# A junk row and two residual rows placed anew at the end of the first attention of a two-layer diffusion trunk

## The chip, the cores and the metric

The kernel runs on one core of one Trainium2 chip, in one launch. The metric is the device time of that core in microseconds (us). Before the change it is 3322.68 us, the median of three runs (3320.38 to 3323.68).

## What is computed

Two layers of a trunk over 1024 latent tokens and 256 context tokens, width 1024, all in float32. Layer 0 mixes grouped-query attention with a bidirectional recurrence; layer 1 is a neighbourhood attention. Each mixer and each gated feed-forward network (a ConvFFN) sits between two RMS norms, with shift, scale and gate from the conditioning vector. The part around the change is the end of layer 0's mixer and the start of its feed-forward network:

```python
y_lat = jnp.concatenate([oa_lat, readout(ob_lat, bg_l)], axis=-1) @ w_out
x = x + g1 * rms_norm(y_lat, norm_post_mix[l])
h_lat = rms_norm(x, norm_pre_ffn[l]) * (1.0 + sc2) + sh2
u = h @ w_up
```

The same is done for the context rows (`ctx`, `h_ctx`). The output is the latent stream after both layers.

## The kernel before, in words

Products run on TensorE (PE) as three products each of operands split into a high and a low part, written in the names as h and l. The program is a row of stages, and each takes its tiles from pools in on-chip memory that are given back when the stage ends. A tile of a later stage that lies on bytes of an earlier one waits for the last instructions that use the earlier tile. In the attention and in the seam behind it the order of each engine, and of the queue of loads on SyncE (SP), is the order in which the code is written (`in_order`).

`even_attention` goes over five blocks of 256 rows, first the context and then four blocks of x, and over 8 heads each. For every pair of block and head, softmax weights `a_p` are computed, turned on PE (`transposes`, L1136) and split into `a_ph0`, `a_pl0`, `a_ph1` and `a_pl1` (halves of the keys), which `values` multiplies into `a_pv`; `finish` adds the two halves of a head by way of `pv_t` into `a_oT` (L1172). The context block has only the first half of the keys.

Between these, `project` multiplies finished blocks by `w_out`, and after the last head it has the engines for itself. For each 128 rows (row tiles 0 to 7 of x, 8 and 9 of the context), `y_half` evicts half a row at a time: a square on ACT with its sum (L354, into a junk row `yjunk`) and a copy on DVE (L355). Then follow the norm (L364), the residual row `y_x`, loaded by SP (L1216) and added (L1222), a store of the sum to `x1d` (L1224), a second square with sum by `squares` (L1191), the row times its inverse norm into `y_x` (L1229), and the store of that to `xnd` (L1230). The stores are issued by GpSimd (POOL). `y_x` has two buffers, so the residual load of row tile n+2 waits for the store of row tile n to `xnd`.

`ffn_up` follows. SP loads the normalised rows back as tiles `n_x` (L1611) in the order 8, 9, 0, 1, 2, 3, then the first two tiles of up-projection weights `w_raw` (L1530), then 4, 5, 6, 7, then the convolution's table `cw` (L1662). PE transposes `n_x` (L1344) into three banks in turn, ACT applies scale and shift (L1345) into `n_t` for the context and `x_t` for the rest, and DVE splits them (L1332, L1333) into `x_ctx` and `x_B` tiles. In the ACT order the first weight cast `w_A11h` (L1546) stands behind the sixth `n_t`; POOL makes its low part (L1547). The first product `u_g` needs four rows of x and these weights.

`squares` writes its squares, which nobody reads, to `sq_junk`, the last small tile at the attention pool's start. In the built program it lies at bytes 21376 to 22400 of each partition, and the place of the first `n_x` tile of the next stage is 20096 to 24192. `a_ph1` and `a_pl1` are each 5120 bytes long, and a row of 1024 values takes 4096.

Of the kernel before, what the change touches and what calls it, by code (L numbers as in the profile page):

```python
# [11 lines left out]
F32 = mybir.dt.float32  # L12
F32R = mybir.dt.float32r
BF16 = mybir.dt.bfloat16
AF = mybir.ActivationFunctionType
# [5 lines left out]
P = 128  # L21
D = 1024
# [17 lines left out]
LINE = 32  # L40
# [25 lines left out]
class Trunk:  # L66
# [958 lines left out]
    def even_attention(self, gp, tp, pp, sp):  # L1025
# [5 lines left out]
        nc, a = self.nc, self.a  # L1031
        QB = 2 * P
        blocks = [(SEQ, 1)] + [(QB * i, 0) for i in range(4)]
# [10 lines left out]
        def load_gate(kind):  # L1044
            g = st["gate"] = sp.tile([P, D], F32, name="gate", bufs=1)
            nc.sync.dma_start(g, self.gated[0, 0, kind].partition_broadcast(P))
# [140 lines left out]
                st["ready"] = b  # L1187

        def squares(y, ms):
            for h in range(2):  # L1190
                nc.scalar.activation(yjunk, y[:, 512 * h:512 * h + 512], AF.Square, scale=1.0 / 32.0, accum_out=ms[:, h:h + 1])  # L1191

        late = []

        def project():

            for b, (n0, kind) in enumerate(blocks):
                for i in range(2):
                    y = sp.tile([P, D], F32, name="y", bufs=2)
                    ms = self.small.tile([P, 2], F32, name="y_ms")  # L1200
                    for half in range(2):
                        ps = gp.tile([P, 512], F32, name="g_ps")
                        for k in range(KT):
                            xhk, xlk = (o[:, i * P:(i + 1) * P] for o in st["o", b, k])
                            whk, wlk = (w[:, 512 * (k % 2):512 * (k % 2) + 512] for w in W[4 * half + k // 2])
                            self.mm(ps, xhk, whk, k == 0, False)
                            self.mm(ps, xhk, wlk, False, False)
                            self.mm(ps, xlk, whk, False, k == KT - 1)
                            if late:
                                late.pop(0)()  # L1210
                            yield b
                        late.append(lambda ps=ps, y=y, ms=ms, half=half: self.y_half(ps, y, ms, half, sp))
                        if half == 0:
                            xt = sp.tile([P, D], F32, name="y_x", bufs=2)
                            r = n0 + i * P
                            nc.sync.dma_start(xt, a["ctx"][i * P:(i + 1) * P] if kind else a["x"][r:r + P])  # L1216
                        else:
                            late.append(lambda ms=ms: st.update(r=self.y_rstd(ms)))
                            late.append(lambda: None)
                            late.append(lambda: None)  # L1220
                            late.append(lambda y=y: self.y_norm(y, st["r"], st["gate"]))
                            late.append(lambda y=y, xt=xt: nc.vector.tensor_tensor(out=y, in0=y, in1=xt, op=OP.add))  # L1222
                            late.append(lambda: None)
                            late.append(lambda y=y, r=r: nc.gpsimd.dma_start(self.x1d[r:r + P], y))  # L1224
                            ms2 = self.small.tile([P, 2], F32, name="y_ms")
                            late.append(lambda y=y, ms2=ms2: squares(y, ms2))
                            late.append(lambda ms2=ms2: st.update(r2=self.y_rstd(ms2)))
                            late.append(lambda: None)
                            late.append(lambda y=y, xt=xt: nc.scalar.mul(xt, y, st["r2"]))  # L1229
                            late.append(lambda xt=xt, r=r: nc.gpsimd.dma_start(self.xnd[r:r + P], xt))  # L1230
                    if b == 0 and i == 1:
                        late.append(lambda: load_gate(0))
            while late:
                late.pop(0)()

        fill, todo, at = project(), [], [0]

        def step(n):
# [5 lines left out]
                elif late:  # L1244
                    late.pop(0)()

        zeros = sp.tile([P, 2 * LINE], F32, name="zeros", bufs=1)[:, 0:1]
        nc.vector.memset(zeros, 0.0)
        pv_t = sp.tile([P, QB], F32, name="pv_t", bufs=1)
        yjunk = sp.tile([P, 512], BF16, name="sq_junk", bufs=1)  # L1250
        N = 2 * len(pairs)
        later = {4: lambda: load_keys(0, 0), 6: lambda: load_keys(0, 1), 8: lambda: load_values(0, NT - 2),
                 10: lambda: load_keys(1, 0), 12: lambda: load_keys(1, 1), 14: lambda: load_gate(1)}
# [1614 lines left out]
```

## Time and profile before

| What | Value |
|---|---|
| Median of three runs | 3322.68 us |
| The profiled execution's own time | 3321.63 us |
| Its span, first to last instruction | 3319.9 us |
| Mean granted TensorE clock | 0.972 |
| Busy: PE, DVE, ACT, POOL | 3097.1, 2019.6, 1502.2, 1562.5 us |
| Main stretch of the first attention | 720 to 1027 us |
| Last projection block alone | 1027 to 1053 us |
| First transposes of the next stage | 1063 us |

The profile is one execution. Busy time is shown by engine; a matmul's end is modelled, so a busy PE isn't PE at its peak. The chain of waits follows the work that ended last back from the end, at each step to what released it. A row of the timeline has the start, the duration, the engine (PEld is the load of weights into PE), the line, the operation, and the tiles written and read; the bracket holds the idle time of that engine just before it and what ended it. A row of a table of waits has the total in us, how many times, and the longest.

### The profile page before, as it was taken

Reading aid. Unit: us, or ns where it says so; the run is one execution under the profiler, and the core shown is the slowest. Engines: PE = TensorE matmul, PEld = TensorE weight load, DVE = VectorE, ACT = ScalarE, POOL = GpSimd, SP = SyncE. Lnnn points to the kernel's source line nnn. Section 1 sums busy time; section 2 is a strip of 40 time slices with the busy share of each in tenths; the row PEclk is TensorE's granted clock in tenths of the full one; section 3 lists DMA queues with packets and bytes.
Section 4 is the critical chain, followed back from the end, with each engine's and each line's share of the span. In section 5 each row is a group of like instructions: output and inputs, shape, how many; then the busy total and the mean of one; then the engine's idle time right before and its main releaser. Section 6 shows DMA issues by size and latency. Waiting matters only on the chain.

```text
span 3319.9 us, 48782 instructions
## 1 busy us (share of the span) xinstructions
PE 3097.1 (93%) x18364; PEld 2547.6 (77%) x18364; DVE 2019.6 (61%) x3386; ACT 1502.2 (45%) x2681; POOL 1562.5 (47%) x1181
## 2 busy tenths in 40 slices
PE   7989999789997899999999989999998989999997
PEld 4766777478886688888878768898986768888785
DVE  4366666567774654554577862477775555555778
ACT  3232232366664543343344442566665434434443
POOL 1130111487773566666510111677764367777202
PEclk8999999889998899999999989999998989999998
DMA  6534311721114121211385772222224212222856
GB/s 249 197 103 133 119 49 38 271 73 60 48 61 153 41 76 69 75 67 66 108 288 195 264 229 107 73 63 61 63 81 155 90 64 88 84 77 89 281 179 218
DMA packets 203357, 398.73 MB, mean 120 GB/s; under 512 B 23521, under 2 KB 85473, under 8 KB 203121
## 3 DMA queue, kind: packets, MB, share of 16 engines
q1 hardware_dynamic: 192512, 358.89, 32.1%
q0 software_dynamic: 10608, 36.72, 2.9%
q8 instruction: 144, 2.36, 0.3%
q14 instruction: 93, 0.75, 0.1%
HBM read 316.86 MB, written 79.06 MB: 119 GB/s over the span
## 4 chain that ended last, share of the span: by engine, by line
PE 72%; DVE 11%; ACT 3%; DMA 3%; issue 3%; POOL 2%; SPq 0%; POOLq 0%; DVEq 0%; ACTq 0%
PE g_ps L136 18%; PE u_g L136 14%; PE d_ps L136 11%; PE u_v L136 10%; PE u_pc L136 4%; PE a_pv L136 2%; PE c_pv L136 2%; PE c_s L136 2%; PE c_pt L2503 2%; PE a_pt L1136 2%; DVE a_pl L1138 1%; PE o_ps L136 1%; PE a_s L136 1%; ACT a_ph L1137 1%; DMA d_rawB<-in_w_down 1%
## 5 line engine op out<-in xcount | busy, mean ns | idle before, releaser
L144 POOL TENSOR_TENSOR rs_r<-rs_e,mhalf 128x1 f32<-128x1 f32 (+3 forms) x106 | 85.7, 809 | 855.7 <-DVE rs_e L143 805.7
L136 PE MATMUL d_ps<-d_Bl,d_Ah 128*128 128x512 f32 x704 | 276.7, 393 | 4.1 <-DVE d_Bl L1874 3.5
L136 PE MATMUL d_ps<-d_Bh,d_Ah 128*128 128x512 f32 x704 | 275.5, 391 | 2.8 <-ACT d_Ah L1873 1.8
L136 PE MATMUL d_ps<-d_Bh,d_Al 128*128 128x512 f32 x704 | 275.7, 392 | 2.0 <-DVE d_Al L1874 1.9
L2486 POOL TENSOR_SCALAR c_p<-c_p,rl 128x640 f32<-128x640 f32 (+1 forms) x128 | 232.5, 1818 | 95.4 <-DVE rl L2485 61.8
L1116 POOL TENSOR_SCALAR a_p<-a_p,rl 128x1280 f32<-128x1280 f32 (+1 forms) x80 | 240.3, 3007 | 55.8 <-DVE rl L1115 49.5
L136 PE MATMUL g_ps<-xh,w_hi 128*128 128x512 f32 (+1 forms) x640 | 256.7, 401 | 5.6 <-DVE hq L748 3.5
L136 PE MATMUL g_ps<-xh,w_lo 128*128 128x512 f32 (+1 forms) x640 | 237.5, 371 | 1.3 <-POOL w_lo L2386 1.3
L136 PE MATMUL g_ps<-xl,w_hi 128*128 128x512 f32 (+1 forms) x640 | 237.7, 371 | 0.0
L1138 DVE TENSOR_TENSOR a_pl<-a_pt,a_ph 128x512 fp32r<-128x512 f32 (+1 forms) x200 | 119.0, 602 | 95.6 <-ACT a_ph L1137 95.5
L1561 DVE TENSOR_TENSOR f_u<-u_v,f_p 128x512 f32<-128x512 f32 x88 | 60.5, 688 | 183.7 <-PE u_v L136 183.7
L1547 POOL TENSOR_TENSOR w_S4l<-w_s,w_S4h 128x512 fp32r<-128x512 f32 x44 | 57.2, 1299 | 229.7 <-ACT w_S4h L1546 229.7
L136 PEld LDWEIGHTS d_ps<-d_Bl,d_Ah 128*128 128x128 f32 x704 | 132.7, 188 | 36.7 <-DVE d_Bl L1874 8.6
L136 PEld LDWEIGHTS d_ps<-d_Bh,d_Ah 128*128 128x128 f32 x704 | 132.8, 189 | 32.6 <-ACT d_Ah L1873 3.1
L136 PEld LDWEIGHTS d_ps<-d_Bh,d_Al 128*128 128x128 f32 x704 | 132.9, 189 | 30.0 <-DVE d_Al L1874 3.3
L1137 ACT CAST a_ph<-a_pt 128x512 fp32r<-128x512 f32 (+1 forms) x200 | 102.0, 518 | 108.6 <-PE a_pt L1136 108.5
L2506 DVE TENSOR_TENSOR c_pl<-c_pt,c_ph 128x256 fp32r<-128x256 f32 (+1 forms) x256 | 112.9, 470 | 57.9 <-ACT c_ph L2505 56.8
L136 PE MATMUL g_ps<-w_hi,xh 128*128 128x512 f32 (+1 forms) x368 | 143.2, 389 | 4.7 <-DVE xh L2260 2.1
L136 PEld LDWEIGHTS g_ps<-xh,w_hi 128*128 128x128 f32 x640 | 121.4, 190 | 31.0 <-issue 14.3
L136 PE MATMUL g_ps<-w_lo,xh 128*128 128x512 f32 (+1 forms) x368 | 137.6, 374 | 4.1 <-DVE w_lo L2247 2.9
L2505 ACT CAST c_ph<-c_pt 128x256 fp32r<-128x256 f32 (+1 forms) x256 | 98.4, 414 | 91.6 <-PE c_pt L2503 89.5
L136 PEld LDWEIGHTS g_ps<-xh,w_lo 128*128 128x128 f32 x640 | 121.0, 189 | 24.1 <-POOL w_lo L2386 1.7
(570 smaller groups left out, 9902.6 us busy)
## 6 DMA issues: line engine op xcount, KB each, us to landing
m_raw<-in_w_mod SPq DMA_DIRECT2D x96, 512.0 KB
w_raw<-in_w_up SPq DMA_DIRECT2D x88, 512.0 KB
d_rawA<-actd SPq DMA_DIRECT2D x77, 512.0 KB
d_rawB<-in_w_down SPq DMA_DIRECT2D x74, 512.0 KB
actd<-f_t SPq DMA_DIRECT2D x22, 640.0 KB
d_t<-in_w_down SPq DMA_DIRECT2D x22, 512.0 KB
actd<-f_t SPq DMA_DIRECT2D x22, 512.0 KB
d_s<-actd SPq DMA_DIRECT2D x20, 512.0 KB
```

The costliest lines, as they stand in the source:

```text
L136: return self.nc.tensor.matmul(out, lhsT, rhs, start=start, stop=stop, skip_group_check=True, **k)
L144: nc.gpsimd.tensor_tensor(out=r[:p, :n], in0=e[:p, :n], in1=self.mhalf[:p, :n], op=OP.pow)
L1116: nc.gpsimd.tensor_scalar(Pt[:, :nk], Pt[:, :nk], rl, None, op0=OP.mult)
L1136: nc.tensor.transpose(pt[:, m, qt * P:(qt + 1) * P], Pt[:, kts[j + m] * P:(kts[j + m] + 1) * P], self.ident)
L1137: nc.scalar.copy(ph[:, j:j + n], pt[:, :n])
L1138: nc.vector.tensor_tensor(out=pl[:, j:j + n], in0=pt[:, :n], in1=ph[:, j:j + n].bitcast(F32), op=OP.subtract)
L1547: nc.gpsimd.tensor_tensor(out=lo, in0=part(j, name), in1=hi.bitcast(F32), op=OP.subtract)
L1561: nc.vector.tensor_tensor(out=out, in0=x, in1=y, op=OP.add)
L2486: nc.gpsimd.tensor_scalar(Pt[:, :n], Pt[:, :n], rl, None, op0=OP.mult)
L2503: nc.tensor.transpose(pt[:, j, :], Pt[:, (src + j) * P:(src + j + 1) * P], self.ident)
L2505: nc.scalar.copy(vap(ph, o, dims), pt[:, :cnt])
L2506: nc.vector.tensor_tensor(out=vap(pl, o, dims), in0=pt[:, :cnt], in1=vap(ph, o, dims).bitcast(F32), op=OP.subtract)
```

## The change

Three edits, all in `even_attention`:

- `squares` no longer has a tile of its own. It takes the tile `yjunk`, the same that `y_half` takes, which lies at the pool's end (byte 153984).
- The residual rows of the last block, row tiles 6 and 7, are put in the places of `a_ph1` and `a_pl1` instead of in the two buffers of `y_x`.
- The tile `zeros` grows from 256 to 768 bytes. With `sq_junk` (1024 bytes) gone, `pv_t` moves up by 512 bytes, and all later tiles of this pool move down by 512.

```diff
         def squares(y, ms):
+            junk = sp.tile([P, 512], BF16, name="yjunk", bufs=1)
             for h in range(2):
-                nc.scalar.activation(yjunk, y[:, 512 * h:512 * h + 512], AF.Square, scale=1.0 / 32.0, accum_out=ms[:, h:h + 1])
+                nc.scalar.activation(junk, y[:, 512 * h:512 * h + 512], AF.Square, scale=1.0 / 32.0, accum_out=ms[:, h:h + 1])

         late = []
+
+        def row_place(b, i):
+            if b < len(blocks) - 1:
+                return sp.tile([P, D], F32, name="y_x", bufs=2)
+            return sp.tile([P, 5 * QB], F32, name="y_x", tag=f"a_p{'hl'[i]}1", bufs=1)[:, :D]
...
-                            xt = sp.tile([P, D], F32, name="y_x", bufs=2)
+                            xt = row_place(b, i)
...
-        zeros = sp.tile([P, 2 * LINE], F32, name="zeros", bufs=1)[:, 0:1]
+        zeros = sp.tile([P, 6 * LINE], F32, name="zeros", bufs=1)[:, 0:1]
...
-        yjunk = sp.tile([P, 512], BF16, name="sq_junk", bufs=1)
```

No instruction is added or removed, and none changes its place in the order of its engine. What changes is what the instructions wait for (and the line numbers behind the edit, by 5 or 6). In the rows below the bracket names the semaphores that an instruction waits for: an engine's own, or DMAHW and DMASW for the transfers that SP and POOL issue. A wait that the engine has already made by an earlier one isn't repeated.

The SP queue before, from the last two residual loads to the `n_x` loads of row tiles 4 and 5:

```order
L1216 DMA y_x<-in_x 128x1024 [waits DMAHW6_49,DMASW5_49,Activation_49]
L1216 DMA y_x<-in_x 128x1024 [waits DMAHW7_49,DMASW7_49,Activation_49]
L1611 DMA n_x<-xnd 128x1024 [waits DMAHW0_49,DVE_49,Activation_49]
L1611 DMA n_x<-xnd 128x1024 [waits DMAHW1_49,PE_49]
L1611 DMA n_x<-xnd 128x1024 [waits DMAHW2_49,Pool_49]
L1611 DMA n_x<-xnd 128x1024 [waits DMAHW3_49]
L1611 DMA n_x<-xnd 128x1024 [waits DMAHW4_49]
L1611 DMA n_x<-xnd 128x1024 [waits DMAHW5_49]
L1530 DMA w_raw<-in_w_up 128x1024 [waits DMAHW6_49,PE_49]
L1530 DMA w_raw<-in_w_up 128x1024 [waits DMAHW7_49]
L1611 DMA n_x<-xnd 128x1024 [waits DMAHW0_49]
L1611 DMA n_x<-xnd 128x1024 [waits DMAHW1_49]
```

The same piece of the SP queue now:

```order
L1222 DMA y_x<-in_x 128x1024 [waits DMAHW6_49,DVE_49,PE_49]
L1222 DMA y_x<-in_x 128x1024 [waits DMAHW7_49,PE_49]
L1616 DMA n_x<-xnd 128x1024 [waits DMAHW0_49,DVE_49]
L1616 DMA n_x<-xnd 128x1024 [waits DMAHW1_49]
L1616 DMA n_x<-xnd 128x1024 [waits DMAHW2_49,Pool_49]
L1616 DMA n_x<-xnd 128x1024 [waits DMAHW3_49]
L1616 DMA n_x<-xnd 128x1024 [waits DMAHW4_49]
L1616 DMA n_x<-xnd 128x1024 [waits DMAHW5_49]
L1535 DMA w_raw<-in_w_up 128x1024 [waits DMAHW6_49,PE_49]
L1535 DMA w_raw<-in_w_up 128x1024 [waits DMAHW7_49]
L1616 DMA n_x<-xnd 128x1024 [waits DMAHW0_49,DMASW5_49]
L1616 DMA n_x<-xnd 128x1024 [waits DMAHW1_49,DMASW7_49]
```

The two residual loads wait for DVE and PE (the last users of `a_ph1` and `a_pl1`) where they waited for the stores of row tiles 4 and 5 (DMASW5 and DMASW7) and for ACT. These two store waits have moved to the loads that read row tiles 4 and 5 back. The first `n_x` load doesn't wait for ACT any more.

ACT before, from the evictions of the last 128 rows to the second `n_t`:

```order
L354 ACTIVATE yjunk,y_ms<-g_ps 128x512 [waits PE_49]
L354 ACTIVATE yjunk,y_ms<-g_ps 128x512 [waits PE_49,Activation_49]
L1191 ACTIVATE sq_junk,y_ms<-y 128x512 [waits DVE_49]
L1191 ACTIVATE sq_junk,y_ms<-y 128x512 [waits Activation_49]
L1229 ACTIVATE y_x<-y,rs_r 128x1024 [waits DMAHW7_49,DMASW7_49,Pool_49]
L1345 ACTIVATE n_t<-n_pv,mod_3_1848,mod_4_3110 128x256 [waits PE_49]
L1345 ACTIVATE n_t<-n_pc,mod_3_1848,mod_4_3110 128x256 [waits PE_49]
```

The same piece of ACT now (x2 is two equal rows):

```order
L354 ACTIVATE yjunk,y_ms<-g_ps 128x512 [waits PE_49,Activation_49] x2
L1192 ACTIVATE yjunk,y_ms<-y 128x512 [waits DVE_49,Activation_49]
L1192 ACTIVATE yjunk,y_ms<-y 128x512 [waits Activation_49]
L1235 ACTIVATE y_x<-y,rs_r 128x1024 [waits DMAHW7_49,Pool_49]
L1350 ACTIVATE n_t<-n_pv,mod_3_1848,mod_4_3110 128x256 [waits DMASW1_49,PE_49]
L1350 ACTIVATE n_t<-n_pc,mod_3_1848,mod_4_3110 128x256 [waits PE_49]
```

Squares and evictions now wait for each other on ACT, since they write one junk row; over the whole program nine ACT instructions get such a wait. The first `n_t` waits for a store (DMASW1, the one of row tile 6 to `xnd`), since it lies on bytes of `a_ph1`, where that row is now. On POOL, the first two sums of weights of the next stage wait likewise for the stores of row tiles 6 and 7.

## The prediction, as it was put on record

> **What bounds the kernel now.** I read the page first, then the stages around the change, then the SP queue's waits, then the chain of waits in order of time, and last the single rows of ACT, DVE, PE and POOL at the one place where these meet.
>
> The page's head and a table by stage (length, then busy time and count of PE, weight loads, DVE, ACT, POOL, then the granted TensorE clock, the DMA share and GB/s):
>
> ```profile
> span 3319.9 us, 48782 instructions
> PE 72%; DVE 11%; ACT 3%; DMA 3%; issue 3%; POOL 2%; SPq 0%; POOLq 0%; DVEq 0%; ACTq 0%
> ...
> 720.00:1027.00 307.00, 284.49 (x1829) 246.65 (x1828) 223.65 (x419) 205.06 (x399) 228.12 (x109) 1.00 0.16 56
> 1027.00:1053.00 26.00, 25.76 (x114) 20.99 (x112) 10.05 (x18) 10.48 (x27) 8.64 (x14) 1.00 0.36 135
> 1053.00:1063.00 10.00, 0.00 (x0) 0.00 (x0) 3.73 (x7) 3.14 (x7) 2.24 (x4) 0.70 0.41 147
> 1063.00:1079.00 16.00, 10.89 (x43) 7.28 (x44) 8.66 (x19) 9.05 (x16) 2.54 (x2) 0.55 1.02 383
> 1130.00:1760.00 630.00, 624.67 (x3197) 534.48 (x3196) 339.59 (x372) 251.32 (x343) 348.15 (x250) 1.00 0.30 105
> ```
>
> TensorE carries 72% of the chain, and from 1130 on it is busy 624.67 of 630 us. The seam between the first attention and the first feed-forward is the exception: PE does nothing from 1053 to 1063, and then, with the DMA share at 1.02, half work at a granted clock of 0.55. The change touches only what comes before this seam, so the question is what the seam waits for. First the SP queue's waits from 1020 to 1110 (in total, times, longest):
>
> ```profile
> SPq L1216 <- DMA xnd<-y_x: 41.3, 2, 30.5
> SPq L1611 <- ACT sq_junk L1191: 15.8, 1, 15.8
> ```
>
> Two residual loads stand still until earlier normalised rows are stored; the third wait is one load of `n_x` (a normalised row tile of the next stage) that waits 15.8 us for `sq_junk`, whose contents nobody reads. In order of time SP, and the chain behind it, look so:
>
> ```profile
> 1031.96 11.55 SPq L1216 DMA_DIRECT2D y_x<-in_x  x2
> 1059.36 3.03 SPq L1611 DMA_DIRECT2D n_x<-xnd  x6
> 1062.49 10.65 DMA w_raw<-in_w_up
> 1074.28 1.02 DVE x_ctx3h L1332
> 1085.18 1.58 DVE x_B211l L1333
> 1086.81 1.81 PE u_g L136 x5
> ```
>
> Six `n_x` loads go out at 1059.36, right behind the last squares, the first up-projection weights at 1062.49 behind them, and their 10.65 us is the longest piece of the chain here. After that DVE alone carries it to 1086.8. ACT and PE, row by row (bracket: idle time and who ended it):
>
> ```profile
> 1049.59 1.15 ACT L1229 ACTIVATE y_x<-y,rs_r 128x1024 f32<-128x1024 f32 x1 [1.12 <-POOL rs_r L144]
> 1050.64 0.58 ACT L354 ACTIVATE yjunk<-g_ps 128x512 bf16<-128x512 f32 x1
> ...
> 1060.45 1.15 ACT L1229 ACTIVATE y_x<-y,rs_r 128x1024 f32<-128x1024 f32 x1 [1.12 <-POOL rs_r L144]
> 1065.23 0.56 ACT L1345 ACTIVATE n_t<-n_pv,mod,mod 128x256 f32<-128x256 f32 x1 [3.63 <-PE n_pv L1344]
> ...
> 1068.83 0.56 ACT L1345 ACTIVATE n_t<-n_pt,mod,mod 128x256 f32<-128x256 f32 x1
> 1073.16 0.62 ACT L1546 CAST w_A11h<-w_raw 128x512 fp32r<-128x512 f32 x1 [3.77 <-DMA w_raw<-in_w_up]
> 1073.69 0.56 ACT L1345 ACTIVATE n_t<-n_pv,mod,mod 128x256 f32<-128x256 f32 x1
> ```
>
> ```profile
> 1052.38 0.39 PE L136 MATMUL g_ps<-w_hi,a_ol 128*128 128x512 f32 x1
> 1063.20 0.45 PE L1344 MATMUL n_pv<-ident,n_x 128*128 128x128 f32 x1 [10.44 <-DMA n_x<-xnd]
> ```
>
> ACT stands idle twice, 3.63 us for transposes that wait for the late `n_x`, 3.77 us for the late weights. Those two holes are what this seam could give back.
>
> **The change, part by part.**
>
> *Junk row.* The squares now write the row that `y_half` uses, at the pool's end, and the first `n_x` tile no longer lies on a row that ACT writes last. In the new order that load waits for DVE alone: of what lies under its tile now (`zeros`, `pv_t`, a part of the keys), `pv_t` is read last, by the last `a_oT` add. The last two residual loads, now in `a_ph1` and `a_pl1`, wait for the last `a_pv` matmuls that read those tiles:
>
> ```profile
> 1026.62 0.28 PE L136 MATMUL a_pv<-a_pl,V 128*128 128x256 f32 x1
> 1027.34 0.42 DVE L1172 TENSOR_TENSOR a_oT<-a_pv,pv_t 64x256 f32<-64x256 f32 x1 [3.17 <-ACT pv_t L1170]
> ```
>
> So SP issues both residual rows at about 1026.9 and six `n_x` at 1027.8 (3.03 us for six issues). They were needed at 1063.2 and took 3.84 us to the first use (1059.36 to 1063.20); even ten times that is hidden under 26 us of projection, where DMA share is 0.36. Both parts are needed: with the junk row alone, SP would be stuck until about 1043 (1031.96 + 11.55) at the second residual load; with the rows alone, `n_x` would still wait for `sq_junk`. The 4 MB that come earlier delay no reader on the path, since PE reads only resident tiles here.
>
> *Weights.* The first two loads still wait for the last projection matmul, 1052.38 + 0.39 = 1052.8. They now stand first instead of behind six others. The worst price I have for them is the 10.65 above, under full DMA load: 1063.5.
>
> *First term.* PE's first transposes need `n_x`, which is there, and a bank that this copy empties:
>
> ```profile
> 1053.58 0.69 DVE L355 COPY y<-g_ps 128x512 f32<-128x512 f32 x1 [1.54 <-ACT yjunk L354]
> ```
>
> They can start at 1054.3 and finish long before ACT is free. ACT is in order and ends `y_x` at 1060.45 + 1.15 = 1061.60; at the same handover above the next instruction begins 0.10 before the end (1050.64 against 1050.74). The first `n_t` moves from 1065.23 to 1061.50: **3.73 us**.
>
> *Second term.* The sixth `n_t` then stands at 1065.10, and the weight cast directly behind it at 1065.10 + 0.56 - 0.10 = 1065.56 instead of 1073.16, since even the worst landing, 1063.5, is earlier. That is another 3.77 + 0.10 = **3.87 us**; together 7.60.
>
> *The collision with POOL.* The low half of the first weights (POOL) will fall nearer to DVE's context splits:
>
> ```profile
> 1069.76 0.42 DVE L1333 TENSOR_TENSOR x_ctx2l<-n_t,x_ctx2h 128x256 fp32r<-128x256 f32 x1
> 1075.32 1.52 DVE L1333 TENSOR_TENSOR x_ctx3l<-n_t,x_ctx3h 128x256 fp32r<-128x256 f32 x1
> ...
> 1073.87 1.26 POOL L1547 TENSOR_TENSOR w_A11l<-w_raw,w_A11h 128x512 fp32r<-128x512 f32 x1 [11.40 <-ACT w_A11h L1546]
> ```
>
> The same operation takes 0.42 alone and 1.52 beside POOL. POOL began 0.71 after the ACT cast, so it will begin at 1066.27, and `x_ctx2l` will run from 1066.03 (1069.76 less 3.73). The overlap costs between 0 and 1.10 us; I take 0.1, near the uncontended row, because DVE starts first. The Trainium skill, page "SBUF — State Buffer", section "Who interferes with whom", says that a VectorE instruction with two SBUF inputs and a GpSimd one that reads SBUF exclude each other, and that whichever issues first keeps the port until it ends. By that rule POOL would wait and the sum would stay at 7.60; by the stretched row alone it would be 6.50. The 1.52 beside POOL agrees with the exclusion; which of the two yields when DVE starts first, no row here shows.
>
> *Own-engine waits.* Sharing the junk row makes nine ACT rows wait for an earlier square on ACT itself. Price: the second square of a pair, which has such a wait already, starts after the one before it has ended, instead of 0.10 before:
>
> ```profile
> 1047.52 0.19 ACT L1191 ACTIVATION_READ_ACCUMULATOR sq_junk<-y 128x1 f32 x1
> 1047.74 0.63 ACT L1191 ACTIVATE sq_junk<-y 128x512 bf16<-128x512 f32 x1
> ```
>
> 1047.74 - 1047.71 + 0.10 = 0.13 us each, 1.2 for nine at most, 0 if other instructions lie between, which they do in the order at all nine. I take 0. Behind them on ACT stand casts of softmax weights, for which PE waits.
>
> *New waits on stores.* The first `n_t` now lies on the row-6 residual and waits until that row is stored; POOL's first sums wait for rows 6 and 7. Landing of these stores, and their issue:
>
> ```profile
> 1051.03 0.57 POOL L1230 DMA_DIRECT2D xnd<-y_x  x1 [1.48 <-ACT y_x L1229]
> 1061.89 0.57 POOL L1230 DMA_DIRECT2D xnd<-y_x  x1 [1.48 <-ACT y_x L1229]
> ...
> DMA to landing us min/median/max: 2.9/3.0/8.2
> ```
>
> Row 6 lands at 1054.0, by the worst store at 1059.2; both are before 1061.50, so the price is 0. If that cover were gone, every microsecond past 1061.50 would go straight into ACT. Row 7 lands at 1064.9 (1070.1 at worst); its `n_x` load is first read in the second half of the rows, where PE stands at
>
> ```profile
> 1082.43 0.60 PE L1344 MATMUL n_pc<-ident,n_x 128*128 128x128 f32 x4
> ```
>
> and 7.5 earlier is 1074.9: 1 us of slack even at worst (1070.1 + 3.84 = 1073.9).
>
> *Addresses.* Nearly all tiles of the attention move 512 bytes down. Nothing in the trace prices an address; I take 0.
>
> *Sum.* 3.73 + 3.87 - 0.1 = **7.5 us**. What follows the seam moves with it: DVE's share of the next stretch (busy time, count, clock, DMA)
>
> ```profile
> 1075.00:1090.00 15.00, 12.61 (x17) 0.84 0.37 144
> ```
>
> is nearly all of it up to 1086.8 (11.8 us), so what moves DVE's start moves PE's `u_g`, and from 1130 on PE is the bound and carries the shift to the end. The profiled execution took 3321.63 us (span 3319.9 and 1.73 around it), 1.05 under the median of the runs: 3321.63 - 7.5 = 3314.1, and from the median 3322.68 - 7.5 = **3315.2 us**.
>
> **Rivals.**
>
> *Only the first hole closes.* If the weights still land late, the cast waits as before: 3322.68 - 3.73 = 3319.0. For it: 10.65 us is a long landing, and DMA share was 1.02. Against: 3 MB of what filled it (six `n_x` of 512 KB) has gone before. Chance 0.08.
>
> *Nothing comes through.* DVE's splits, or the last row's `n_x`, set the seam's end: 3322.7. For it: that row's load needs the store after the last squares, which does not move. Against: 1 us of slack at the worst landing and 6 at the usual. Chance 0.06.
>
> *More than the sum.* PE at 0.55 of its clock runs a part of its 10.89 us in the seam faster, since its first transposes now stand before 1056; a quarter of 10.89 is 2.7, so 3312.5. Against: it will still idle some 6 us until 1061.5, and DVE is the bound there. Chance 0.08.
>
> *Slower: the new wait takes the place of the old.* The row-6 store now shares the DMA engines with the weights issued at 1052.8, and the first `n_t`, with all of ACT behind it, waits for it. It eats the gain when it lands later than 1061.5 + 7.5 = 1069.0, 18 us after its issue, and costs a microsecond for each one after that; at 25 us in flight the kernel takes 3329.7. Against: the slowest such store took 8.2 us, against six loads and two more. Chance 0.04.
>
> **How the numbers follow.** The forecast has 0.74, with its own range of 3313.4 to 3317.4: above, the collision's other end (1.0 more) and the nine waits (1.2); below, the collision's 0.1 and half of the 3.3 us by which the three runs differ. To leave out no more than 2 in 10 the range reaches to the partial gain and to the larger one: **3312.4 to 3319.1**. A measurement of this kernel can tell about 0.2% from no change, 6.6 us: the line is at 3316.0, only 0.8 above the forecast. Faster by more: three quarters of the forecast's 0.74 plus the 0.08 for more, rounded: 0.64. Within 0.2%: the rest of it, the partial gain and the absorbed one: 0.32. Slower by more: 0.04.
>
> **What would show it.** Right: `n_x` issued near 1028; the first weights cast directly behind the sixth `n_t`, near 1065.6, with no wait for a DMA; PE's first transposes near 1054.4; `u_g` reaching x_B211l near 1079.3; all later stages as long as before. Wrong: ACT's first `n_t` released by a store; `w_A11h` still released by `w_raw`; a second-half transpose waiting for `n_x`; or an attention of other than 307 us up to the last `a_pv`.

## The result, and the profile after

The changed kernel takes **3314.24 us** in the median of 11 runs (3309.9 to 3321.32); the kernel before, run beside it, 3323.68 us. The ratio is 0.9972, with a 95% interval of 0.9964 to 0.998: between 6.6 and 12.0 us faster. The forecast was 3315.2, with 7.5 us gained. Run once more later, the changed kernel gave 3315.85 and a ratio of 0.9978 (0.9969 to 0.9986).

The single profiled execution took 3309.9 us, 11.7 less than the profiled one of before, and is the fastest of its eleven. It can't be compared as a whole, so I measure the seam by itself: **from the start of ACT's last multiplication into `y_x` to the start of PE's `u_g<-x_B211l`**. Before, by the rows shown in the prediction, that is 1086.81 - 1060.45 = 26.36 us. After:

```profile
1059.51 1.15 ACT L1235 ACTIVATE y_x<-y,rs_r 128x1024 f32<-128x1024 f32 x1 [1.12 <-POOL rs_r L144]
1060.57 0.55 ACT L1350 ACTIVATE n_t<-n_pv,mod,mod 128x256 f32<-128x256 f32 x1
...
1064.14 0.56 ACT L1350 ACTIVATE n_t<-n_pt,mod,mod 128x256 f32<-128x256 f32 x1
1064.61 0.61 ACT L1551 CAST w_A11h<-w_raw 128x512 fp32r<-128x512 f32 x1
```

```profile
1053.33 0.44 PE L1349 MATMUL n_pv<-ident,n_x 128*128 128x128 f32 x2 [1.56 <-DVE y L355]
...
1078.29 0.50 PE L136 MATMUL u_g<-x_B211l,w_A12h 128*128 128x512 f32 x1 [1.17 <-DVE x_B211l L1338]
```

1078.29 - 1059.51 = **18.78 us: 7.58 less**. Both holes on ACT are gone (no bracket at the end of the row of the first `n_t` and none at `w_A11h`), and PE's first transposes run seven microseconds before ACT is free for them. The SP queue shows why (start, length, count):

```profile
1025.82 0.81 SPq L1222 DMA_DIRECT2D y_x<-in_x  x2
1026.79 2.85 SPq L1616 DMA_DIRECT2D n_x<-xnd  x6
1051.80 1.03 SPq L1535 DMA_DIRECT2D w_raw<-in_w_up  x2
1052.93 12.62 SPq L1616 DMA_DIRECT2D n_x<-xnd  x4
```

The six `n_x` go out 32.6 us earlier than before. The stages, in the columns of the prediction's table:

```profile
720.00:1027.00 307.00, 284.58 (x1828) 246.72 (x1827) 223.08 (x417) 204.48 (x399) 227.88 (x108) 1.00 0.17 56
1027.00:1053.00 26.00, 24.77 (x110) 20.18 (x108) 10.05 (x18) 10.50 (x27) 8.62 (x14) 1.00 0.68 262
1053.00:1063.00 10.00, 2.39 (x12) 1.50 (x12) 5.03 (x13) 4.38 (x9) 2.27 (x4) 0.62 0.96 344
1063.00:1079.00 16.00, 13.86 (x64) 10.05 (x63) 15.28 (x24) 13.01 (x22) 6.92 (x5) 0.81 0.26 85
```

The attention (first row) is unchanged. In the second row the DMA share is 0.68 instead of 0.36: the transfer now lies beside the projection. In the last row DVE is busy 15.28 of 16 us. The chain of waits, which ran through a 10.65 us weight load, now runs through DVE (start, length, what):

```profile
1052.18 6.00 DMA w_raw<-in_w_up
...
1065.71 1.07 DVE x_ctx3h L1337
1066.81 1.50 DVE x_ctx3l L1338
...
1072.75 2.38 DVE x_B210l L1338 x2
1075.13 1.44 DVE x_B211h L1337
1076.66 1.58 DVE x_B211l L1338
1078.29 1.74 PE u_g L136 x5
```

What lies outside the seam? When the instructions of ACT are matched one by one, after stands 0.94 us earlier than before just ahead of the seam, 8.53 behind it, and 11.72 at the end. The second profile of the changed kernel stands 4.97 us *later* ahead of the seam, 2.62 earlier behind it, and 5.12 at the end. The step at the seam is the same in both, 7.59; the other steps come and go, so I take them for scatter between runs.

One of them can be read. It lies in the five microseconds from `u_g` on, here for the kernel before and for the first and the second profile of the changed one (columns as above):

```profile
1086.81:1091.81 5.00, 5.00 (x24) 4.57 (x25) 2.47 (x4) 1.55 (x2) 0.00 (x0) 0.66 0.00 0
1078.29:1083.29 5.00, 5.00 (x24) 4.55 (x25) 2.53 (x4) 1.55 (x2) 0.00 (x0) 0.66 0.00 0
1084.18:1089.18 5.00, 5.00 (x37) 4.72 (x38) 2.52 (x4) 2.07 (x3) 0.60 (x1) 1.00 0.00 0
```

The granted clock is 0.66 in the first two and 1.00 in the third, where PE gets through 37 matmuls instead of 24 and reaches its next wait for ACT 10.11 us after `u_g` instead of 11.72: 1.61 us less. The kernel with the residual rows alone, whose seam is that of before, has the 1.00 and the 10.11 too, so this step does not belong to the change. It is one way in which a whole time can gain more or less than the seam.

### The profile page after: what moved, and what is told of

It reads as the page before. It is cut to its first block, busy times and chain, and to the rows that moved or that the text cites. A ratio compares the mean times of both kernels' runs of the same rounds, so it can differ in the third digit from the quotient of the medians.

```text
span 3308.1 us, 48791 instructions
## 1 busy us (share of the span) xinstructions
PE 3097.5 (94%) x18364; PEld 2547.4 (77%) x18364; DVE 2018.8 (61%) x3386; ACT 1501.6 (45%) x2681; POOL 1560.7 (47%) x1181
## 4 chain that ended last, share of the span: by engine, by line
PE 73%; DVE 11%; ACT 3%; DMA 3%; issue 3%; POOL 1%; SPq 0%; DVEq 0%; ACTq 0%; POOLq 0%
PE g_ps L136 19%; PE u_g L136 14%; PE d_ps L136 11%; PE u_v L136 10%; PE u_pc L136 4%; PE a_pv L136 2%; PE c_pv L136 2%; PE c_s L136 2%; PE c_pt L2508 2%; PE a_pt L1136 2%; DVE a_pl L1138 1%; PE a_s L136 1%; PE o_ps L136 1%; DMA m_raw<-in_w_mod 1%; ACT a_ph L1137 1%
```

## The experiments

Medians, ratios to the kernel before beside which each ran (with intervals), and the seam of each profiled execution:

| kernel | median us | ratio (95%) | seam us |
|---|---|---|---|
| before | 3323.42 to 3324.83 | 1 | 26.36 |
| changed | 3314.24 | 0.9972 (0.9964-0.9980) | 18.78 |
| junk row alone | 3314.19 | 0.9967 (0.9955-0.9979) | 18.78 |
| residual rows alone | 3325.12 | 0.9999 (0.9990-1.0008) | 26.27 |
| own junk row, two lines of zeros | 3320.48 | 0.9983 (0.9974-0.9991) | 18.77 |
| before, weights first | 3319.83 | 0.9982 (0.9973-0.9990) | 22.07 |
| changed, weights last | 3320.29 | 0.9995 (0.9986-1.0004) | 23.04 |
| changed, two lines of zeros | 3320.31 | 0.9986 (0.9977-0.9995) | 18.78 |
| changed, POOL sums later | 3314.42 | 0.9978 (0.9969-0.9987) | 16.45 |
| junk row alone, POOL sums later | 3312.38 | 0.9969 (0.9958-0.9979) | 16.44 |
| the same, low halves on DVE | 3313.91 | 0.9970 (0.9959-0.9980) | 16.10 |
| changed, again | 3315.85 | 0.9978 (0.9969-0.9986) | 18.76 |

In the two profiles of the changed kernel and in the three kernels that leave its seam as it is, the seam agrees within 0.02 us, while whole times scatter by ten: the seam decides about steps, the medians about the total.

### The junk row alone

```diff
 def row_place(b, i):
...
-    return sp.tile([P, 5 * QB], F32, name="y_x", tag=f"a_p{'hl'[i]}1", bufs=1)[:, :D]
+    return sp.tile([P, D], F32, name="y_x", bufs=2)
```

> The junk row alone: squares on the shared row at the pool's end, but the last block's residual rows stay in the two ordinary row buffers. Theory of the prediction (both parts are needed): the queue stands at the second residual load until about 1043, the six n_x loads come too late, and less than half of the seam's gain is left (seam of 22.6 us or more, against 26.4 before and 18.8 after; time within 3.7 us of before). Rival (the junk row alone suffices): n_x go out at 1043.6, land by about 1053, before PE's first transposes are due, the weights still stand first, and the whole gain stays: seam 18.8 us (at most 1 more), time as the changed kernel's, some 9 us under before.

This kernel keeps the longer `zeros` tile; what that does is taken alone further down, and it leaves the seam at 18.78.

The rival is right, and my prediction's sentence was wrong. SP does stand at the second residual load, then sends everything in time (SP queue):

```profile
1034.05 11.61 SPq L1222 DMA_DIRECT2D y_x<-in_x  x2
1045.75 2.94 SPq L1616 DMA_DIRECT2D n_x<-xnd  x6
1054.88 0.83 SPq L1535 DMA_DIRECT2D w_raw<-in_w_up  x2
```

This execution runs 3.1 us later than the changed one ahead of the seam; the first `n_t` still begins 1.06 us after the last `y_x` (1062.59 and 1063.65), and the seam is 18.78. In the seam as it is now, the new place of the residual rows is worth nothing.

### The residual rows alone

The kernel before with the new `row_place` and nothing else of the change.

> The residual rows alone: the last block's rows lie in places of the turned softmax weights, the squares keep sq_junk under the first n_x tile. Both theories: the two residual loads go out near 1027, but n_x still wait for the last squares, go out near 1059.4 and hold back ACT's first n_t (idle about 3.6 us) and the first weight cast: seam 26.4 us, time within 1 us of before. A third theory (the queue alone is what counts, so an early residual load is worth something by itself) would give a seam of 25 us or less.

Confirmed. SP and ACT:

```profile
1031.85 0.81 SPq L1221 DMA_DIRECT2D y_x<-in_x  x2
1064.39 3.17 SPq L1616 DMA_DIRECT2D n_x<-xnd  x6
```

```profile
1070.65 0.56 ACT L1350 ACTIVATE n_t<-n_pv,mod,mod 128x256 f32<-128x256 f32 x1 [4.01 <-PE n_pv L1349]
...
1078.11 0.62 ACT L1551 CAST w_A11h<-w_raw 128x512 fp32r<-128x512 f32 x1 [3.30 <-DMA w_raw<-in_w_up]
```

The residual loads go early, `n_x` wait for the junk row instead, and both holes stand. SP's wait (total, times, longest):

```profile
SPq L1616 <- ACT sq_junk L1191: 31.6, 1, 31.6
```

### A junk row of the squares' own

```diff
-junk = sp.tile([P, 512], BF16, name="yjunk", bufs=1)
+junk = sp.tile([P, 512], BF16, name="sq_junk", bufs=1)
...
-zeros = sp.tile([P, 6 * LINE], F32, name="zeros", bufs=1)[:, 0:1]
+zeros = sp.tile([P, 2 * LINE], F32, name="zeros", bufs=1)[:, 0:1]
```

> The changed kernel with a junk row of the squares' own at the pool's end, so that no square waits for a square of another helper on ACT. Theory (the nine own-engine waits cost nothing): seam 18.8 us, attention before it as long as in the changed kernel to 0.3 us, time the same within 0.1%. Rival (0.13 us each come through): up to 1.2 us faster than the changed kernel, and the shift grows by steps of 0.13 through the attention.

The seam is the same (18.77) and the attention from 715 to 1040 keeps its shift against the changed kernel to 0.1 us, so the nine own-engine waits cost nothing. The total is not as either theory had it: 3320.48, 4.6 to 6.2 us slower than the two medians of the changed kernel. The loss, 8.7 us in this profile, lies at 600 to 690, far from the squares. This kernel also has the shorter `zeros` tile, which the next section takes alone. That the seam is 18.77 here as well shows one thing more: what closes the holes is the new place of the junk row, not that it is shared.

### Two lines of zeros

```diff
-zeros = sp.tile([P, 6 * LINE], F32, name="zeros", bufs=1)[:, 0:1]
+zeros = sp.tile([P, 2 * LINE], F32, name="zeros", bufs=1)[:, 0:1]
```

> The changed kernel with the zeros tile back at two lines instead of six, so that all tiles behind it lie 512 bytes lower; nothing else. Theory, from the run with a junk row of its own: at these addresses the first key load of the attention lies on a modulation row and waits for DVE to write that row, so the stretch from 590 to 690 grows by 4 to 9 us, the seam stays at 18.8, and the time is 4 to 8 us above the changed kernel, as with the own junk row (3320.5). Rival (addresses cost nothing, the own row or chance made that run slower): time as the changed kernel's, 3314, and no long wait of the first key load.

The theory holds: 3320.31, seam 18.78. The first key load of the attention, without a wait in the changed kernel, now has one (SP's waits: total, times, longest; the kernel with the own junk row has the same 12.0), and PE waits for what is queued behind it:

```profile
SPq L1070 <- DVE mod L339: 12.0, 1, 12.0
```

```profile
641.78 0.60 PE L311 MATMUL mod_pt<-ident,mod_rows 128*128 128x128 f32 x4
647.58 1.19 PE L136 MATMUL g_ps<-K_0c,a_q 128*128 128x256 f32 x4 [5.19 <-DMA a_q<-q2d]
```

In the changed kernel the same two rows are 0.35 us apart instead of 5.80:

```profile
635.77 0.60 PE L311 MATMUL mod_pt<-ident,mod_rows 128*128 128x128 f32 x4
636.12 0.72 PE L136 MATMUL g_ps<-K_0c,a_q 128*128 128x256 f32 x4
```

With 512 bytes less in front of it, the tile of `K_0c` comes to lie on a row `mod` that DVE writes late. So the four extra lines in the diff, which I had priced at zero, keep off a loss of 4.5 to 6 us in the medians (3320.31 against 3315.85 and 3314.24). They bring nothing against before, where this wait does not exist either.

This profile loses 9.4 us against the changed kernel's from 600 to 690. The wait is about 5 of them. About 4 are something else: PE stands still in the middle of 32 small matmuls, with no releaser that the profile shows.

```profile
606.95 0.38 PE L136 MATMUL h_pa<-hQ,hKM 128*32 128x32 f32 x21 [0.36 <-ACT hKM L802]
610.94 0.37 PE L136 MATMUL h_pa<-hQ,hKM 128*32 128x32 f32 x10 [3.61 <-issue]
```

The same place shows 3.33 us with the own junk row, 2.23 with the weights last and 2.51 with the POOL sums later, and no such stall in the others. The last two kernels differ from the changed one only behind the attention, and neither profile of the changed kernel has the stall, so the layout does not make it by itself. What it is stays open, and so does its share in the medians; no run separates it.

### The weights first, in the kernel before

```diff
 for i, t in tags.items():
-    if i == 4:
+    if i == 8:
         load(0, 0)
         load(0, 1)
```

(`tags` begins with row 8, so the two weight loads now come before the first `n_x`. In the trace a third one, of the next piece, follows directly behind them, 5.6 us before the first `n_x`.)

> The kernel before with one edit: the first two weight loads stand ahead of the n_x loads in the queue, so they no longer come behind six of them; n_x still wait for sq_junk. Theory (two independent holes on ACT): the second hole closes and the first stays, seam 26.4 - 3.9 = 22.5 us, ACT's first n_t still near 1065. Rival (one shared cause, the late n_x with a full DMA): n_x behind the weights come even later, ACT's first hole grows by what the second loses, seam 25 us or more.

Two independent holes: the seam is 22.07, 4.29 less, where 3.9 was expected. ACT:

```profile
1066.27 0.56 ACT L1345 ACTIVATE n_t<-n_pv,mod,mod 128x256 f32<-128x256 f32 x1 [3.33 <-PE n_pv L1344]
...
1070.33 0.61 ACT L1546 CAST w_A11h<-w_raw 128x512 fp32r<-128x512 f32 x1
```

The first hole stays (3.33 us), the second is gone. What then separates this kernel from the changed one, 22.07 - 18.78 = 3.29, is about the hole that is left (3.33).

### The weights last, in the changed kernel

```diff
 for i, t in tags.items():
-    if i == 4:
-        load(0, 0)
-        load(0, 1)
     xs[i] = hp.tile([P, D], F32, name="n_x", tag=t, bufs=1)
     nc.sync.dma_start(xs[i], self.xnd[i * P:(i + 1) * P])
+load(0, 0)
+load(0, 1)
```

> The changed kernel with the first two weight loads behind all ten n_x loads in the queue, so they wait for the store of the last residual row. Theory (the second hole on ACT is set by the landing of the weights alone): ACT's first n_t stays early (1.06 us after the last y_x begins, as in the changed kernel), w_A11h waits for its load again and falls 3 to 3.5 us later, seam 22 to 22.3 us, time 3 to 3.5 us above the changed kernel. Rival (the 10.65 us landing of the kernel before came from the full DMA, not from the place in the queue; issued behind a mere four n_x loads the weights land in about 4 us): seam 20 us or less.

The counterpart: first hole closed, second open (the third load in the row is again one of the next piece).

```profile
1070.29 1.34 SPq L1535 DMA_DIRECT2D w_raw<-in_w_up  x3
```

```profile
1066.51 0.55 ACT L1350 ACTIVATE n_t<-n_pv,mod,mod 128x256 f32<-128x256 f32 x1
...
1074.83 0.62 ACT L1551 CAST w_A11h<-w_raw 128x512 fp32r<-128x512 f32 x1 [4.18 <-DMA w_raw<-in_w_up]
```

The seam is 23.04, 4.26 longer, where 3.2 to 3.5 was expected, and the median 3320.29 is 4.4 to 6.1 above the changed kernel's, where 3 to 3.5 was expected. The rival has half a point: from issue to the cast it is 4.54 us here, against 10.67 before, so the long landing of before goes with the six `n_x` still in flight in front. But the place in the queue decides all the same: SP stands 10.3 us at the last `n_x` until its row is stored, and the loads behind it go out at 1070.29, when ACT could cast near 1070.6 (0.47 after the start of its last `n_t`).

### POOL's sums later

In the changed kernel four steps of the seam move behind the first group of the second half: a weight split (ACT cast and POOL subtraction) and two sums on POOL.

```diff
-split(0, "A21")
...
-total(0, "S1", "A21", OP.add, "A22")
-total(0, "S2", "S1", OP.subtract, "A11")
 for i, _ in enumerate(second_half):
     if i == 0:
         product(st["G", 0][:, :512], ("A12",), "B21", False, True)
+        split(0, "A21")
+        total(0, "S1", "A21", OP.add, "A22")
+        total(0, "S2", "S1", OP.subtract, "A11")
```

> The changed kernel with three POOL operations of the seam (the low half of one weight and two weight sums) and the ACT cast ahead of them issued after the second group of context rows instead of before it. Theory (POOL stretches DVE's splits beside it, 2.38 against 1.29 and 2.17 against 1.29 and 1.50 against 0.42 us, and DVE is what PE waits for): the splits fall back to their short times, seam 15.8 to 16.8 us, time 2 to 3 us below the changed kernel. Rival 1 (the sums come late for TensorE): the seam shrinks but PE then waits for a weight sum, and nothing is left at 1130. Rival 2 (the stretch comes with something other than POOL): the splits stay long, seam 18.8.

DVE and PE of this kernel:

```profile
1081.42 1.29 DVE L1338 TENSOR_TENSOR x_B210l<-x_t,x_B210h 128x512 fp32r<-128x512 f32 x2
1083.19 0.43 DVE L1337 CAST x_B211h<-x_t 128x512 fp32r<-128x512 f32 x1 [0.47 <-ACT x_t L1350]
1083.72 1.48 DVE L1338 TENSOR_TENSOR x_B211l<-x_t,x_B211h 128x512 fp32r<-128x512 f32 x2
```

```profile
1084.63 0.40 PE L136 MATMUL u_g<-x_B211l,w_A12h 128*128 128x512 f32 x1
```

2.38, 1.50 and 2.17 us have become 1.29, 0.43 and 1.48; PE no longer waits at `x_B211l`, and the seam is 16.45, 2.33 shorter. The ACT cast that left has a part in it, since DVE now waits 0.47 for ACT; no run separates that. Behind the seam the first rival is partly right, for POOL is late with the weights that stand behind the moved sums:

```profile
1091.71 0.50 PE L136 MATMUL u_g<-x_B110h,w_A11l 128*128 128x512 f32 x1 [0.65 <-POOL w_A11l L1552]
```

From ahead of the seam to 1163 the matched instructions gain 2.99 us on the first profile of the changed kernel, but only 0.93 on the second, which like this one has the granted clock of 1.00 behind the seam. So a part of the 2.33 is lost again; the three profiles with this clock and a seam of 18.8 differ by no more than 0.34 at 1163. The median does not show the rest: 3314.42, where 2 to 3 us less was expected, with an interval that overlaps that of the changed kernel.

### Junk row alone with the sums later, the low halves on DVE, and the changed kernel again

The first is the last kernel with `row_place` as in the junk row alone. The second also hands the low halves of the first two weights to DVE:

```diff
-def split(j, name):
+def split(j, name, low=nc.gpsimd):
...
-        nc.gpsimd.tensor_tensor(out=lo, in0=part(j, name), in1=hi.bitcast(F32), op=OP.subtract)
+        low.tensor_tensor(out=lo, in0=part(j, name), in1=hi.bitcast(F32), op=OP.subtract)
...
-    split(0, "A11")
+    split(0, "A11", nc.vector)
...
-    split(0, "A12")
+    split(0, "A12", nc.vector)
```

> The junk row alone (residual rows in the ordinary row buffers) together with the POOL operations issued later. Theory (both effects hold by themselves and add): seam 16.5 us, time 2 to 3 us under the changed kernel run beside it. Rival (the later loads of the ordinary row buffers matter once the seam is shorter): seam 17 us or more, with a wait for n_x or for w_raw on ACT or PE.

> The last kernel, and the two low halves of the first weights computed by DVE instead of POOL. Theory (POOL beside DVE costs DVE more than the work itself: the stretched cast and split lose 0.77 + 1.08 us to two POOL operations, while DVE's own subtraction of that size takes about 0.69, so 1.4 for both): x_ctx3h back to 0.29 and x_ctx3l to 0.42 us, seam 0.4 to 0.7 us shorter (15.8 to 16.1), if nothing else is next. Rival (the seam is then bound by TensorE at a low clock and by ACT, not by DVE): DVE is ahead but the seam stays at 16.4.

> The changed kernel once more, on the same chip as the two versions that should beat it. Seam 18.8 us again; by the theory that the steps of the shift outside the seam are chance, the shift against the kernel before has other steps at other places than the first time, between -3 and +9 us ahead of the seam, and the same 7.6 at it.

All three ran on one chip. The first has a seam of 16.44 and a median of 3312.38, 3.5 under the changed kernel beside it (3315.85): both effects hold without the new place of the residual rows. At 1163 it has 1.43 us more than this second profile of the changed kernel. Its ratio of 0.9969 (0.9958 to 0.9979) still overlaps that of the changed kernel (0.9969 to 0.9986), so the times alone do not prove it the faster; they go the way of the seam. The second, on DVE and PE:

```profile
1066.65 0.68 DVE L1552 TENSOR_TENSOR w_A11l<-w_raw,w_A11h 128x512 fp32r<-128x512 f32 x1
1067.25 0.29 DVE L1337 CAST x_ctx3h<-n_t 128x256 fp32r<-128x256 f32 x1
1067.58 0.42 DVE L1338 TENSOR_TENSOR x_ctx3l<-n_t,x_ctx3h 128x256 fp32r<-128x256 f32 x1
```

```profile
1070.65 0.65 PE L1349 MATMUL n_pc<-ident,n_x 128*128 128x128 f32 x4 [0.28 <-ACT x_t L1350]
```

DVE does POOL's work in 0.68 and is ahead nevertheless, but the seam gains only 0.34 (16.10), just under the expected 0.4: PE waits 0.28 for ACT in the row above and for nothing from there to `u_g<-x_B211l`, as the rival said in part. Its time, 3313.91, is not to be told from the one before. The changed kernel again has the seam of 18.76 and other steps elsewhere, as expected.

## Why the prediction was right, and where it was not

**The first term (3.73 us): right.** `n_t` follows the start of the last `y_x` by 1.06 us, after 4.78 before: 3.72. The cause is the junk row alone (18.78 with it, 26.27 with the residual rows).

**The second term (3.87 us): right.** From the first `n_t` to `w_A11h` it was 7.93 and is 1060.57 to 1064.61, 4.04: 3.89. The weights landed at 1052.18 + 6.00 = 1058.2, well under the 1063.5 allowed for; the six `n_x` that stood in front of them before had gone out 25 us earlier. Each hole is confirmed by a kernel that closes it alone. With the weights last only the first closes: 26.36 - 23.04 = 3.32, and the hole left open is 4.18 there instead of 3.77, so 0.41 comes back: 3.73. With the weights first only the second closes: 26.36 - 22.07 = 4.29, and the first hole is 3.33 there instead of 3.63; less these 0.30 it is 3.99.

**The collision (0.1, between 0 and 1.10): right.** DVE and POOL of the changed kernel:

```profile
1065.07 0.43 DVE L1338 TENSOR_TENSOR x_ctx2l<-n_t,x_ctx2h 128x256 fp32r<-128x256 f32 x1
1065.71 1.06 DVE L1337 CAST x_ctx3h<-n_t 128x256 fp32r<-128x256 f32 x1 [0.22 <-ACT n_t L1350]
```

```profile
1065.31 1.32 POOL L1552 TENSOR_TENSOR w_A11l<-w_raw,w_A11h 128x512 fp32r<-128x512 f32 x1 [3.75 <-ACT w_A11h L1551]
```

POOL begins while `x_ctx2l` runs; `x_ctx2l` keeps its 0.43. `x_ctx3h` starts while POOL runs and takes 1.06 instead of 0.29: it ends at 1066.77, just behind POOL (1066.63). The Trainium skill, page "SBUF — State Buffer", section "Who interferes with whom", says that whichever issues first keeps the shared ports for the whole instruction; both DVE rows agree. How long POOL waited for `x_ctx2l` no row shows: its 1.32 us are only 0.05 more than its next subtraction takes (1.27). What the sum did not ask is what POOL beside DVE still costs elsewhere in the seam: 2.33 us with the two sums and the split, 0.34 more with the first low halves. It was the same before, so the forecast did not suffer.

**Own-engine waits (0), new waits on stores (0): right.** The own junk row left seam and attention alike. The first `n_t` has no idle time ahead of it, so the store of row 6 was done; the second-half transposes, from 1073.90 on, wait for no `n_x`.

**Addresses (0): right for the change as a whole, by a step I did not take.** I priced a shift of 512 bytes at nothing and did not ask why `zeros` grows. Without that, tiles move 1024 bytes, and a key load waits 12.0 us for DVE: 4.5 to 6 us of the gain would be gone. The address itself cost nothing that shows here; it decided which tile lies under which, and so who waits for whom.

**"Both parts are needed": wrong in its first half.** I had the right figure, SP stuck until 1043, and did not carry it on: 3.03 us for the six issues and a landing of 3.84 end near 1050, before the first transposes at 1054.4 have a bank, and 11 us before ACT is free. With the rows alone nothing comes, as I said; with the junk row alone everything does.

**The rivals.** Only one hole, nothing, and a new wait on a store did not happen. Neither did the larger gain by a faster PE clock, inside the seam. From 1063 to 1079 the granted clock did rise from 0.55 to 0.81, but other work stands in that window now: counted back from `u_g<-x_B211l` it is 0.50 from 17 to 10 us ahead and 0.97 in the last 10, before and after. The seam gained what ACT's holes measure.

**The total: right, and closer than it had to be.** The seam's 7.58 us is what the sum forecast. That the first median, 3314.24, lies within 1 us of 3315.2 is partly luck: the medians gain 9.4 and 7.8 us, and steps like the 1.61 behind the seam come and go. The intervals of the times, 6.6 to 12.0 us and 4.7 to 10.3, both hold 7.6.

## What to carry to other kernels

Before pricing a load that waits, write down when it would be needed, and price only what comes after that: here a wait of 11.6 us was free and one of 15.8 cost two holes, the second through the loads queued behind it. A buffer that nobody reads still holds up the load that is placed over it, and in a full memory any tile that moves may come to lie under another load; list the waits of the new layout at all places, also far from the change. After a hole is closed, look for who carries the chain next: it was DVE beside POOL, worth another 2.33 us of the seam. Then look further on: against the second profile of the changed kernel, 0.93 and 1.43 us of it were left 80 us later.

## What the runs showed of the hardware

A single-input cast on DVE (128x256, f32 to fp32r) is held up by POOL's subtraction just as a two-input one is: 1.06 us against 0.29. An operation of 1.3 us on POOL cost DVE 0.77 us (the cast) and 1.07 us (`x_ctx3l`, 1.50 against 0.43), where DVE needs 0.68 us to do the same work itself. The same matmuls right behind the seam ran at a granted clock of 0.66 in three profiles and of 1.00 in the other nine, the two profiles of one kernel among both. And PE can stand still for 2.2 to 3.6 us in a row of equal small matmuls with nothing that the profile names as the cause, always behind the 21st of 32, in four of the twelve profiles.
